# Hybrid diffusion trunk on one core: thirteen up blocks of each layer by seven products, their weight sums by adding transfers, and modulation vectors made beside merge and output projection

## The chip, the core and the metric

The kernel runs on one core of a Trainium2 chip. The core has a matrix engine (TensorE; PE in the profile, and PEld for its loading of weights), a vector engine (VectorE; DVE), a scalar engine (ScalarE; ACT), a general engine (GpSimd; POOL) and a queue that issues transfers (SyncE; SP), all running side by side and waiting for one another by semaphores. The metric is the device time of one run in microseconds; less is better.

## The reference, cut to what matters

There are 640 tokens of 1024 channels: 128 of a context (segment 0, modulated by `c_ctx`) and 512 latent ones (segment 1, modulated by `c`). Two layers do this (cut):

```
mods = silu(cond) @ w_ada[l] + b_ada[l]              # sh1, sc1, g1, sh2, sc2, g2: 6 x 1024, per segment
hn   = rmsnorm(x, norm1_g) * (1 + sc1) + sh1
f, q, k, v, gates = split(hn @ w_in)
a_four = real(fft2(f)) @ w_fourier                   # 512 -> 1024
a_attn = subln(diff_attention(q, k, v)) @ w_attn     # 1024 -> 1024
x  = x + g1 * ((sigmoid(gates)[:D] * a_four + sigmoid(gates)[D:] * a_attn) @ w_o)
hn = rmsnorm(x, norm2_g) * (1 + sc2) + sh2
u  = dwconv3(hn @ w_up, conv_w, conv_b)              # 1024 -> 2 x 2816, then 3 taps over the tokens
x  = x + g2 * ((silu(u[gate half]) * u[value half]) @ w_down)
```

All of it is float32.

## The kernel before, in words

**Layout and precision.** Channels lie on the 128 partitions and tokens on the free axis: a tile of x is 128 channels x 640 tokens, and there are eight. All large products go over float32 values that are split into a high part and a low part: `split` writes a tile's high part on ACT and its low part on DVE. One k step of an output tile is then three products for each half of the tokens (320 columns): high by high, high by low, low by high. One such product is a line `MATMUL ... 128x320` in the profile.

**Weights.** All weights of both layers are one stream of blocks in the order in which they are used (`make_plan`): `wf` (Fourier projection), `wa` (attention projection), `wo` (output projection), `up` (2 x 11 in each layer: g = 0 the value half, g = 1 the gate half, j = 0 to 10, two output tiles each), `dn` (down projection). A block of 1 MB lies in one of two buffers `w_raw` and is loaded by SP (`pump_loads`) when the block two ahead of it has been split. `queue_split` cuts it into pieces of 512 columns: ACT casts the high part into one of eight buffers `w_h`, DVE subtracts it into `w_l`. The pieces are emitted one at a time between the products (`tick`), no more than eight ahead.

**Blocks by seven products.** An ordinary up block makes two output tiles over two halves of the tokens in 2 x 2 x 8 x 3 = 96 products. Seen as a 2 x 2 matrix of quarters (`r11`, `r12`, `r21`, `r22`: output tile by half of k) it can be done in seven products of quarters instead of eight: 7 x 4 x 3 = 84. `seven` does this, with sums of `hn` tiles that are made once in a layer (`sums`) and with sums of weight quarters that `queue_split` makes for each block: `s3` = r11 + r21, r21 += r22, `s2` = r21 + r11, and later s2 += r12: four additions of DVE. Then DVE and ACT combine the seven results (`r0`, `r1`). `seven(l, g, j)` tells which blocks go this way: before, in layer 1, those of g = 0 with j of 3 and up. A layer that has such blocks is `fast`: its convolution goes over all 640 tokens in two taps, with the edge at token 128 mended by ACT.

**Down rounds.** When some up blocks are done, the finished tiles of the hidden layer are multiplied with their part of w_down (`FF_ROUNDS`: from which tile, and how many; `FF_AFTER`: behind which j). Layer 0 has three rounds (8, 6 and 8 tiles), layer 1 four (4, 6, 6 and 6). The last round of a layer is skewed with the norm of the next.

**Modulation vectors.** w_ada comes in blocks of eight k steps. `ada_open(upto, rate)` allows blocks up to a number and sets how many steps are done at each `tick`; `ada_load` has SP load 256 KB into a ring of four tiles; a step (`ada_step`) is two `SCALAR_TENSOR_TENSOR` operations of DVE, 128 x 512, `acc += w * c`, one for each segment. After each pair of blocks TensorE sums over partitions (`ada_rows`) and transposes (`ada_columns`). `ada_until` does at once what is left. The numbers `ADA_UPTO` say for each layer up to which block this goes beside the gate projection, and up to which beside the up projection.

**The norm between output projection and up projection.** `w_o` and `up_first` overlap: the second half of the tokens' output projection runs while the first half's norm is made, and the first up block is done on the first half while the second half's norm is made. For each half: sums of squares on ACT and DVE, their sum on TensorE, `ms` on DVE, `rs` = ms ** -0.5 on POOL (L597), rows of it on TensorE, then for each of the eight tiles a multiplication, on POOL the modulation (L632), and the split.

**What sets the order.** The Python code gives the order in the main. A scheduler of the tile framework then orders the instructions of each engine, and puts in the waits for tiles; buffers named `slot` come from a pool of 61.

Of the kernel before, what the change touches and what calls it, by code (L numbers as in the profile page):

```python
# [34 lines left out]
ADA_UPTO = ((6, 14), (20, 20))  # L35
ADA_RATE = (.85, .25)
FF_ROUNDS = (((0, 8), (8, 6), (14, 8)), ((0, 4), (4, 6), (10, 6), (16, 6)))
FF_AFTER = ((4, 7, 10), (2, 5, 8, 10))


def seven(l, g, j):

    return l == 1 and g == 0 and j >= 3
# [37 lines left out]
def make_plan():  # L81
# [16 lines left out]
    for l in range(DEPTH):  # L98
        kq(l, 0)
        v(l, 0)  # L100
        for h in range(8):
            if h < 7:
                kq(l, h + 1)
                if h < 6 and h % 2 == 0:
                    v(l, h // 2 + 1)
            else:
                for i in range(2):
                    w(("f", l, i), "w_in", l, 0, 8, [(256 * i, 256)])
        for i in range(4):
            for g in range(2):  # L110
                w(("g", l, g, i), "w_in", l, 0, 8, [(3584 + 1024 * g + 256 * i, 256)])
        for i in range(2):
            w(("wf", l, i), "w_fourier", l, 0, 4, [(512 * i, 512)])
        for i in range(4):
            w(("wa", l, i), "w_attn", l, 0, 8, [(256 * i, 256)])
        for i in range(4):
            w(("wo", l, i), "w_o", l, 0, 8, [(256 * i, 256)])

        def up(j):
            for g in range(2):  # L120
                add(("up", l, g, j), "s" if seven(l, g, j) else "w", "w_up", l, 0, 8, [(DFF * g + 256 * j, 256)])

        def down(r):
            m0, n = FF_ROUNDS[l][r]
            for i in range(4):
                w(("dn", l, r, i), "w_down", l, 128 * m0, n, [(256 * i, 256)])

        for j in range(11):
            up(j)
            if j in FF_AFTER[l]:  # L130
                down(FF_AFTER[l].index(j))
# [67 lines left out]
class Kern:  # L199
# [123 lines left out]
    def pump_loads(self, upto=None):  # L323
        while self.loaded < (upto or self.n) and (self.loaded < 2 or self.done[self.loaded - 2]):
            i = self.loaded
            n = self.plan[i][2][0] * self.plan[i][2][1]
            src = self.I["w_stream"][self.woff[i]:self.woff[i + 1]].rearrange("(p n) -> p n", n=n)
            self.nc.sync.dma_start(out=self.raw[i % 2][:, 0:n], in_=src)
            self.loaded += 1

# [8 lines left out]
    def queue_split(self, j):  # L339
# [19 lines left out]
        if self.plan[i][3] == "s":  # L359
            r11, r12, r21, r22 = (raw[:, 512 * q:512 * q + 512] for q in range(4))  # L360
            s3, s2 = (t[:, 0:512] for t in self.st)

            def plus(out, a, b, g):
                self.split_q.append((g, lambda: nc.vector.tensor_add(out=out, in0=a, in1=b)))

            part(g0, r11)
            plus(s3, r11, r21, g0 + 1)
            plus(r21, r21, r22, g0 + 1)
            plus(s2, r21, r11, g0 + 1)
            part(g0 + 1, s2)  # L370
            part(g0 + 2, s3)
            plus(s2, s2, r12, g0 + 3)
# [751 lines left out]
    def up(self, l, j, hn):  # L1124
        yv = {}
        for g in range(2):
            W = self.begin("up", l, g, j)
            if g and j in FF_AFTER[l] and self.fast:
                self.bg.extend(self.split_early(l, FF_AFTER[l].index(j)))
# [85 lines left out]
    def ff_split(self, l, r):  # L1215

        m0, n = FF_ROUNDS[l][r]
# [5 lines left out]
    def split_early(self, l, r):  # L1223

        m0, n = FF_ROUNDS[l][r]
# [14 lines left out]
    def down_last(self, l, after_a):  # L1240
        r = len(FF_ROUNDS[l]) - 1
# [231 lines left out]
    def layer(self, l, hn, hooks_b):  # L1473
# [74 lines left out]
        self.ada_open(ADA_UPTO[l][0], ADA_RATE[0])  # L1548
# [22 lines left out]
        self.finish_a(l, 1)  # L1571
        Z = self.merge(l)
# [3 lines left out]
        self.ada_open(ADA_UPTO[l][1], ADA_RATE[1])  # L1576
        self.ff = [None] * NFF
        if self.fast:
            self.st = [self.alloc(), self.alloc()]
# [3 lines left out]
        for j in range(1, 11):  # L1583
# [4 lines left out]
            if j in FF_AFTER[l][:-1]:  # L1588
                self.ada_until(8)
                self.down(l, FF_AFTER[l].index(j))  # L1590
        for pr in hn2:
            self.give(*pr)
        if self.fast:
            self.give(*self.st)
            for pr in self.t13 + self.t24:
                self.give(*pr)
        if l + 1 < DEPTH:
            self.ada_until(ADA_UPTO[l][1])
# [53 lines left out]
```

## Time and profile before

| | |
|---|---|
| median of 3 runs | 2190.96 us (2189.55 to 2192.48) |
| profiled execution: its own time | 2191.04 us |
| its span, first to last instruction | 2189.3 us |
| mean granted clock of TensorE | 0.994 of full speed |
| TensorE busy | 2139.6 us, 98% of the span |
| DVE busy | 1439.9 us, 66% |
| ACT busy | 988.2 us, 45% |
| POOL busy | 236.0 us, 11%, 348 instructions |
| HBM read | 194.64 MB |

The time is that of the whole run; the span leaves out the little that lies around the instructions. Busy shares are averages over stages with different limits. Stages are found in the trace by the weight blocks: each product names its weight buffer, so the first product of a block is known from the order of the plan.

### The profile page before, as it was taken

To read this page: it belongs to the slowest core of one execution; us is meant where nothing else is said; L and a number is where in the kernel's file an instruction comes from. 1 tells how busy PE (TensorE), PEld (TensorE's weight loads), DVE (VectorE), ACT (ScalarE), POOL (GpSimd) and SP (SyncE) were. 2 spreads that over 40 slices of the span, in tenths; PEclk is the share of its full clock that TensorE was granted. 3 is DMA by queue.
4 is the path that set the end of the run, shared out by engine and by line. 5 is a ranking of instruction groups with operands and counts; after the bars stand their busy time and mean duration, and the time that the engine had idled before them with its cause. 6 is when DMAs were issued, how large, how long until landed. Compare 5 with 4: busy or idle time off the path is not lost.

```text
span 2189.3 us, 36833 instructions
## 1 busy us (share of the span) xinstructions
PE 2139.6 (98%) x14766; PEld 2077.3 (95%) x14766; DVE 1439.9 (66%) x2562; ACT 988.2 (45%) x2015; POOL 236.0 (11%) x348
## 2 busy tenths in 40 slices
PE   8999999999999999999999999999999999999997
PEld 5999989999999999999999999899999999999997
DVE  5776678744479856655466776695544776857574
ACT  4665654342245423323356666543422563525352
POOL 2122222000030000000041222120000300000001
PEclk9999999999999999999999999999999999999998
DMA  8211114522234423232211111154222122222221
GB/s 319 71 51 59 48 41 153 171 82 77 91 117 140 136 97 120 93 106 92 78 68 66 45 48 56 60 159 158 78 78 77 54 84 76 78 78 82 73 78 49
DMA packets 59787, 201.74 MB, mean 92 GB/s; under 512 B 6624, under 2 KB 14176, under 8 KB 44768
## 3 DMA queue, kind: packets, MB, share of 16 engines
q1 hardware_dynamic: 59616, 199.39, 27.2%
q8 instruction: 116, 1.90, 0.4%
q14 instruction: 55, 0.45, 0.1%
HBM read 194.64 MB, written 4.72 MB: 91 GB/s over the span
## 4 chain that ended last, share of the span: by engine, by line
PE 78%; DVE 7%; ACT 6%; POOL 5%; issue 4%; DMA 1%; SPq 0%; ACTq 0%; DVEq 0%; POOLq 0%
PE ps_d L296 43%; PE ps_s L296 17%; PE ps_t L296 17%; ACT slot L188 4%; DVE slot L188 3%; POOL ors L858 2%; PE ps_t L300 2%; POOL slot L632 2%; DVE nm L188 1%; DVE on L188 1%; ACT junk L188 1%; POOL oms L857 1%; DVE w_l L188 1%; ACT w_h L188 0%; POOL slot L890 0%
## 5 line engine op out<-in xcount | busy, mean ns | idle before, releaser
L296 PE MATMUL ps_d<-slot,w_h 128*128 128x320 f32 x4984 | 983.1, 311 | 4.3 <-DVE slot L188 4.2
L296 PEld LDWEIGHTS ps_d<-slot,w_h 128*128 128x128 f32 x4984 | 787.5, 188 | 15.5 <-DVE slot L188 7.2
L296 PE MATMUL ps_d<-slot,w_l 128*128 128x320 f32 x2492 | 596.3, 309 | 1.7 <-DVE w_l L188 1.6
L188 ACT CAST w_h<-w_raw 128x512 fp32r<-128x512 f32 x520 | 318.8, 621 | 461.4 <-PE ps_d L296 240.2
L188 DVE TENSOR_TENSOR w_l<-w_raw,w_h 128x512 fp32r<-128x512 f32 x520 | 354.6, 690 | 153.4 <-ACT w_h L188 150.4
L296 PEld LDWEIGHTS ps_d<-slot,w_l 128*128 128x128 f32 x2492 | 423.2, 188 | 2.3 <-DVE w_l L188 2.3
L188 DVE TENSOR_TENSOR slot<-slot,slot 128x640 f32<-128x640 f32 (+5 forms) x339 | 240.1, 715 | 100.2 <-ACT slot L188 70.2
L296 PE MATMUL ps_t<-slot,w_h 128*128 128x320 f32 x1384 | 277.5, 309 | 0.6 <-DVE slot L188 0.3
L296 PE MATMUL ps_s<-slot,w_h 128*128 128x320 f32 x1376 | 264.9, 309 | 0.0
L296 PEld LDWEIGHTS ps_t<-slot,w_h 128*128 128x128 f32 x1384 | 221.1, 187 | 7.0 <-issue 2.5
L296 PEld LDWEIGHTS ps_s<-slot,w_h 128*128 128x128 f32 x1376 | 218.8, 188 | 0.8 <-issue 0.8
L188 DVE SCALAR_TENSOR_TENSOR slot<-slot,c_cond,slot 128x512 f32<-128x512 f32 x280 | 199.0, 746 | 29.5 <-DMA slot<-in_w_ada 20.2
L188 ACT ACTIVATE slot<-ps_s,nm 128x640 f32<-128x640 f32 (+1 forms) x160 | 113.6, 710 | 161.2 <-DVE nm L188 160.1
L296 PE MATMUL ps_t<-slot,w_l 128*128 128x320 f32 x692 | 175.4, 308 | 0.0
L296 PE MATMUL ps_s<-slot,w_l 128*128 128x320 f32 x688 | 164.2, 308 | 0.0
L188 ACT ACTIVATE slot<-slot 128x640 f32<-128x640 f32 (+2 forms) x132 | 85.1, 647 | 144.2 <-DVE slot L188 141.9
L188 DVE TENSOR_REDUCE nm<-ps_s 128x1 f32<-128x640 f32 (+1 forms) x160 | 113.8, 711 | 50.3 <-PE ps_s L296 43.8
L188 ACT CAST slot<-slot 128x640 fp32r<-128x640 f32 (+1 forms) x156 | 112.4, 726 | 49.5 <-DVE slot L188 47.4
L296 PE MATMUL ps_s<-slot,slot 128*128 128x320 f32 (+2 forms) x592 | 114.7, 318 | 5.5 <-ACT slot L188 4.7
L296 PEld LDWEIGHTS ps_t<-slot,w_l 128*128 128x128 f32 x692 | 120.1, 187 | 0.0
L296 PEld LDWEIGHTS ps_s<-slot,w_l 128*128 128x128 f32 x688 | 117.3, 188 | 0.0
L597 POOL TENSOR_TENSOR rs<-ms,c_mh 128x3 f32<-128x3 f32 (+1 forms) x9 | 8.6, 955 | 951.8 <-DVE ms L188 951.8
(142 smaller groups left out, 2199.1 us busy)
## 6 DMA issues: line engine op xcount, KB each, us to landing
w_raw<-in_w_stream SPq DMA_DIRECT2D x116, 1024.0 KB, 4.9
slot<-in_w_ada SPq DMA_DIRECT2D x160, 256.0 KB, 2.9
w_raw<-in_w_stream SPq DMA_DIRECT2D x16, 768.0 KB, 4.3
slot<-in_w_first SPq DMA_DIRECT2D x32, 256.0 KB, 6.3
slot<-in_x_t SPq DMA_DIRECT2D x8, 320.0 KB, 5.6
slot<-in_t_big SPq DMA_DIRECT2D x10, 256.0 KB, 4.1
out_y_t<-slot SPq DMA_DIRECT2D x8, 320.0 KB, 2.2
w_raw<-in_w_stream SPq DMA_DIRECT2D x4, 512.0 KB, 3.7
```

The source lines that it names most:

```text
L188: return f(*a, **kw)
L296: return self.nc.tensor.matmul(**a)
L300: return self.nc.tensor.transpose(*a)
L597: nc.gpsimd.tensor_tensor(out=rs[:, 0:n], in0=ms[:, 0:n], in1=self.mh[:, 0:n], op=ALU.pow)
L632: (eng or nc.gpsimd).tensor_scalar(out=tmp[:, a:b], in0=tmp[:, a:b], scalar1=A, scalar2=B, op0=ALU.mult, op1=ALU.add)
L857: nc.gpsimd.tensor_scalar(out=ms, in0=ss, scalar1=1.0 / 128, scalar2=EPS, op0=ALU.mult, op1=ALU.add)
L858: nc.gpsimd.tensor_tensor(out=rs, in0=ms, in1=self.mh[:, 0:1], op=ALU.pow)
```

## The change

It has four parts. In each layer 13 blocks go by seven products: those of g = 0 with j of 3 and up, and those of g = 1 with j of 3, 4, 6, 7 and 9. Their weight sums are no longer made by DVE from the loaded block: `sum_weights`, called where the block's load is issued, has SP load r11 once more into s2 and s3, and has POOL issue four transfers that add as they arrive (`accum_op`): r22 to the loaded r21, r21 to s3, r21 to s2, r22 to s2. The two sum tiles are doubled, as the weight buffers are. One addition (s2 += r12) stays on DVE. Layer 0 is now `fast` also, and takes layer 1's four down rounds. The second part of the modulation blocks is opened ahead of `merge`, at .85 steps a tick in layer 0 and .3 in layer 1, and is done by the end of `w_o`; nothing of it stands beside the up blocks any more.

```
-ADA_UPTO = ((6, 14), (20, 20))
-ADA_RATE = (.85, .25)
-FF_ROUNDS = (((0, 8), (8, 6), (14, 8)), ((0, 4), (4, 6), (10, 6), (16, 6)))
-FF_AFTER = ((4, 7, 10), (2, 5, 8, 10))
+ADA_UPTO = ((6, 12), (18, 20))
+ADA_RATE = ((.85, .85), (.85, .3))
+FF_ROUNDS = ((0, 4), (4, 6), (10, 6), (16, 6))
+FF_AFTER = (2, 5, 8, 10)
 def seven(l, g, j):
-    return l == 1 and g == 0 and j >= 3
+    return g == 0 and j >= 3 or j in (3, 4, 6, 7, 9)
...
-            self.nc.sync.dma_start(out=self.raw[i % 2][:, 0:n], in_=src)
+            raw = self.raw[i % 2]
+            self.nc.sync.dma_start(out=raw[:, 0:n], in_=src)
+            if self.plan[i][3] == "s":
+                self.sum_weights(i, raw, src)
             self.loaded += 1
+
+    def sum_weights(self, i, raw, src):
+
+        nc = self.nc
+        r11, r12, r21, r22 = (slice(512 * q, 512 * q + 512) for q in range(4))
+        s3, s2 = (t[:, 0:512] for t in self.st[i % 2])
+        for t, q in ((s2, r11), (s3, r11)):
+            nc.sync.dma_start(out=t, in_=src[:, q])
+        for t, q in ((raw[:, r21], r22), (s3, r21), (s2, r21), (s2, r22)):
+            nc.gpsimd.dma_start(out=t, in_=src[:, q], accum_op=ALU.add)
...
-            s3, s2 = (t[:, 0:512] for t in self.st)
-
-            def plus(out, a, b, g):
-                self.split_q.append((g, lambda: nc.vector.tensor_add(out=out, in0=a, in1=b)))
...
+            s3, s2 = (t[:, 0:512] for t in self.st[i % 2])
...
             part(g0, r11)
-            plus(s3, r11, r21, g0 + 1)
-            plus(r21, r21, r22, g0 + 1)
-            plus(s2, r21, r11, g0 + 1)
             part(g0 + 1, s2)
             part(g0 + 2, s3)
-            plus(s2, s2, r12, g0 + 3)
+            self.split_q.append((g0 + 3, lambda: nc.vector.tensor_add(out=s2, in0=s2, in1=r12)))
             part(g0 + 3, r21)
...
-        self.ada_open(ADA_UPTO[l][0], ADA_RATE[0])
+        self.ada_open(ADA_UPTO[l][0], ADA_RATE[l][0])
...
         self.finish_a(l, 1)
+        self.ada_open(ADA_UPTO[l][1], ADA_RATE[l][1])
         Z = self.merge(l)
...
         hooks = self.w_o(l, Z, hn2)
-        self.ada_open(ADA_UPTO[l][1], ADA_RATE[1])
+        self.ada_until(ADA_UPTO[l][1])
...
         if self.fast:
-            self.st = [self.alloc(), self.alloc()]
+            self.st = [[self.alloc(), self.alloc()] for _ in range(2)]
...
-                self.ada_until(8)
```

TensorE's list has 13,947 instructions after and 14,163 before. What the change does to the order of instructions is shown at three places.

The first is POOL's list between the two halves of layer 0's second norm: the modulation of the first half (`slot` tiles, 128 x 128 and 128 x 192), then `rs` of the second half, then its modulation (128 x 320). Before:

```order
L632 TENSOR_SCALAR slot26_6577<-slot26_6577,c_a01_81,c_mods0_78 128x128 [waits PE_49,Activation_49]
L632 TENSOR_SCALAR slot26_6577<-slot26_6577,c_a01_81,c_mods0_78 128x192 [waits Activation_49]
L632 TENSOR_SCALAR slot27_6584<-slot27_6584,c_a01_81,c_mods0_78 128x128 [waits Activation_49]
L632 TENSOR_SCALAR slot27_6584<-slot27_6584,c_a01_81,c_mods0_78 128x192 [waits Activation_49]
L597 TENSOR_TENSOR rs_6747<-ms_6746,c_mh_75 128x3 [waits DVE_49]
L632 TENSOR_SCALAR slot18_6770<-slot18_6770,c_a01_81,c_mods0_78 128x320 [waits Activation_49]
```

Of the same place after, where `slot50` and `slot40` are the two s2 tiles and `slot31` and `slot34` the two s3 tiles (lines L342, L604 and L639 are the adding transfer, `rs` and the modulation):

```order
L639 TENSOR_SCALAR slot32_6758<-slot32_6758,c_a01_81,c_mods0_78 128x128 [waits PE_49,Activation_49]
L639 TENSOR_SCALAR slot32_6758<-slot32_6758,c_a01_81,c_mods0_78 128x192 [waits Activation_49]
L342 DMA slot50_6853<-in_w_stream 128x512 [waits DMAHW7_49,PE_49]
L639 TENSOR_SCALAR slot36_6765<-slot36_6765,c_a01_81,c_mods0_78 128x128 [waits Activation_49]
L639 TENSOR_SCALAR slot36_6765<-slot36_6765,c_a01_81,c_mods0_78 128x192 [waits Activation_49]
L342 DMA slot50_6853<-in_w_stream 128x512 [waits DMASW0_49]
L342 DMA slot40_6851<-in_w_stream 128x512 [waits DMAHW1_49,DVE_49]
L342 DMA slot31_6850<-in_w_stream 128x512 [waits DMAHW2_49]
L342 DMA slot34_6852<-in_w_stream 128x512 [waits DMAHW3_49,DVE_49]
L342 DMA slot40_6851<-in_w_stream 128x512 [waits DMASW2_49]
L604 TENSOR_TENSOR rs_6934<-ms_6933,c_mh_75 128x3 [waits DVE_49]
L639 TENSOR_SCALAR slot12_6713<-slot12_6713,c_a01_81,c_mods0_78 128x320 [waits Activation_49]
```

Six transfers of two blocks' sums have moved in between, and the second addition into a tile waits there for the landing of the first (`DMASW`).

The second place is DVE's list in the attention projection of layer 0: `slot45` and `slot47` are attention gates that are multiplied with a projected tile `ps_d`, `slot28` and `slot48` the sums Z, `w_l3` a weight split. Before:

```order
L188 TENSOR_TENSOR slot45_4452<-slot45_4452,ps_d_5675 128x640 [waits PE_49]
L188 TENSOR_TENSOR w_l3_103<-w_raw0_90,w_h3_95 128x512 [waits Activation_49]
L188 TENSOR_TENSOR slot28_4276<-slot28_4276,slot45_4452 128x640 [waits DVE_49]
L188 TENSOR_TENSOR slot31_5748<-slot28_4276,slot23_5747 128x640 [waits Activation_49]
L188 TENSOR_TENSOR slot47_4727<-slot47_4727,ps_d_5730 128x640 [waits PE_49]
```

And after, where the rows with `c_cond` are modulation steps:

```order
L188 TENSOR_TENSOR slot45_4452<-slot45_4452,ps_d_5715 128x640 [waits PE_49]
L188 TENSOR_TENSOR w_l3_103<-w_raw0_90,w_h3_95 128x512 [waits Activation_49]
L188 TENSOR_TENSOR slot28_4276<-slot28_4276,slot45_4452 128x640 [waits DVE_49]
L188 SCALAR_TENSOR_TENSOR slot17_5952<-slot29_5346,c_cond_77,slot17_5952 128x512
L188 SCALAR_TENSOR_TENSOR slot57_5951<-slot39_5343,c_cond_77,slot57_5951 128x512 [waits DMAHW5_49]
L188 TENSOR_TENSOR slot16_5796<-slot28_4276,slot38_5795 128x640 [waits Activation_49]
L188 SCALAR_TENSOR_TENSOR slot17_5952<-slot39_5343,c_cond_77,slot17_5952 128x512 [waits DVE_49]
L188 SCALAR_TENSOR_TENSOR slot57_5951<-slot13_5344,c_cond_77,slot57_5951 128x512 [waits DMAHW6_49,DVE_49]
L188 SCALAR_TENSOR_TENSOR slot17_5952<-slot13_5344,c_cond_77,slot17_5952 128x512 [waits DVE_49]
L188 SCALAR_TENSOR_TENSOR slot57_5951<-slot33_5345,c_cond_77,slot57_5951 128x512 [waits DMAHW7_49,DVE_49]
L188 TENSOR_TENSOR slot47_4727<-slot47_4727,ps_d_5778 128x640 [waits PE_49]
```

Between two tiles of the projection DVE now has six such steps.

The third place is DVE's list where a seven block's weights are split. Before (layer 1; `slot37` is s2, `slot14` and `slot59` are tiles of the convolution, `slot4` and `slot5` of x):

```order
L188 TENSOR_TENSOR w_l4_104<-w_raw0_90,w_h4_96 128x512 [waits PE_49,Activation_49]
L188 TENSOR_TENSOR w_raw0_90<-w_raw0_90 128x512
L188 SCALAR_TENSOR_TENSOR slot5_127<-ps_d_18222,c_mods1_79,slot5_127 128x128 [waits PE_49]
L188 SCALAR_TENSOR_TENSOR slot5_127<-ps_d_18222,c_mods1_79,slot5_127 128x512
L188 TENSOR_TENSOR slot37_17330<-w_raw0_90 128x512 [waits DVE_49]
L188 TENSOR_TENSOR w_l5_105<-slot37_17330,w_h5_97 128x512 [waits Activation_49]
L188 TENSOR_TENSOR slot37_17330<-slot37_17330,w_raw0_90 128x512 [waits DVE_49]
```

And after (layer 0; `slot50` is s2, `slot34` s3, `slot36` and `slot58` take the combined products):

```order
L188 TENSOR_TENSOR w_l7_107<-w_raw1_91,w_h7_99 128x512 [waits DMAHW4_49,Activation_49]
L188 TENSOR_TENSOR w_l0_100<-slot50_6853,w_h0_92 128x512 [waits DMASW1_49,PE_49,Activation_49]
L188 TENSOR_TENSOR slot50_6853<-slot50_6853,w_raw1_91 128x512 [waits DVE_49]
L188 TENSOR_TENSOR slot36_7968<-slot36_7968,ps_s_7966 128x320 [waits PE_49,Activation_49]
L188 TENSOR_TENSOR w_l1_101<-slot34_6852,w_h1_93 128x512 [waits DMASW4_49,Activation_49]
L188 TENSOR_TENSOR slot58_7969<-ps_t_7967,slot36_7968 128x320 [waits DVE_49,PE_49]
L188 TENSOR_TENSOR w_l2_102<-w_raw1_91,w_h2_94 128x512 [waits DMASW7_49,Activation_49]
```

The additions ahead of the split of s2 are gone, and the splits of s2, s3 and r21 wait for a POOL transfer's landing instead.

## Rows read from the trace of the kernel before

**Rows 1.** The page: TensorE's busy time, and the last chain's shares by engine.

```profile
PE 2139.6 (98%) x14766; PEld 2077.3 (95%) x14766; DVE 1439.9 (66%) x2562; ACT 988.2 (45%) x2015; POOL 236.0 (11%) x348
...
PE 78%; DVE 7%; ACT 6%; POOL 5%; issue 4%; DMA 1%; SPq 0%; ACTq 0%; DVEq 0%; POOLq 0%
```

**Rows 2.** Stretches, layer 0: length, busy by engine, clock, DMA share, GB/s.

```profile
726.68:742.40 15.72, 15.72 (x110) 14.68 (x110) 14.55 (x26) 7.33 (x12) 0.00 (x0) 1.00 0.48 139
756.46:784.62 28.16, 28.16 (x195) 28.16 (x193) 23.54 (x41) 11.39 (x18) 0.00 (x0) 1.00 0.44 150
```

**Rows 3.** Stretches: layer 1's eight seven blocks (PE, PEld, DVE, ACT, POOL).

```profile
1858.82:1871.34 12.52, 12.52 (x86) 12.33 (x85) 10.48 (x18) 6.37 (x13) 0.00 (x0) 1.00 0.41 151
...
2007.88:2020.65 12.77, 12.77 (x86) 12.34 (x85) 9.53 (x16) 6.49 (x13) 0.00 (x0) 1.00 0.17 63
...
sum 101.46, PE 101.46 PEld 98.67 DVE 81.20 ACT 48.70 POOL 0.00; mean PE 12.68 PEld 12.33 DVE 10.15 ACT 6.09 POOL 0.00
```

**Rows 4.** Stretches: output projection to second up pair; layer 0's first up block.

```profile
604.10:684.40 80.30, 76.66 (x506) 75.91 (x505) 66.81 (x127) 40.15 (x72) 21.55 (x26) 0.96 0.37 119
633.60:656.30 22.70, 19.06 (x111) 18.31 (x110) 16.25 (x32) 8.96 (x17) 11.15 (x15) 0.85 0.41 139
1686.30:1761.60 75.30, 74.57 (x506) 73.09 (x505) 54.82 (x104) 41.55 (x84) 21.85 (x26) 1.00 0.21 71
```

**Rows 5.** TensorE's waits, 633 to 660: total us, times, longest.

```profile
PE ps_s L296 <- POOL rs L597: 2.8, 1, 2.8
```

**Rows 6.** POOL's timeline at the second norms of both layers (start, duration).

```profile
623.03 1.29 POOL L597 TENSOR_TENSOR rs<-ms,c_mh 128x3 f32<-128x3 f32 x1 [243.17 <-DVE ms L188]
...
1710.00 11.26 POOL L632 TENSOR_SCALAR slot<-slot,c_a,c_mods 128x128 f32<-128x128 f32 x16 [4.23 <-ACT slot L188]
1725.75 0.86 POOL L597 TENSOR_TENSOR rs<-ms,c_mh 128x3 f32<-128x3 f32 x1 [4.49 <-DVE ms L188]
```

**Rows 7.** Timeline, 1105 to 1128: one issue of SP.

```profile
1111.26 0.33 SPq L665 DMA_DIRECT2D slot<-in_k_t  x1
```

**Rows 8.** The page: transfers, KB each, median us from issue to landing.

```profile
w_raw<-in_w_stream SPq DMA_DIRECT2D x116, 1024.0 KB, 4.9
slot<-in_w_ada SPq DMA_DIRECT2D x160, 256.0 KB, 2.9
...
slot<-in_w_first SPq DMA_DIRECT2D x32, 256.0 KB, 6.3
```

**Rows 9.** Stretch: merge and first half of layer 0's output projection.

```profile
491.00:604.10 113.10, 113.10 (x775) 113.09 (x773) 54.83 (x79) 28.62 (x46) 0.00 (x0) 1.00 0.24 82
```

**Rows 10.** DVE by shape, 491 to 633.6: busy us, mean ns, idle before.

```profile
L188 DVE TENSOR_TENSOR w_l<-w_raw,w_h 128x512 fp32r<-128x512 f32 x36 | 24.7, 690 | 14.0 <-ACT w_h L188 14.0
L188 DVE TENSOR_TENSOR slot<-slot,slot 128x640 fp32r<-128x640 f32 x12 | 9.8, 823 | 3.2 <-ACT slot L188 3.2
L188 DVE SCALAR_TENSOR_TENSOR slot<-slot,c_cond,slot 128x512 f32<-128x512 f32 x13 | 9.3, 742 | 1.6 <-ACT slot L188 1.6
```

**Rows 11.** Stretch of layer 1's first up blocks, where DVE is fullest.

```profile
1738.70:1763.70 25.00, 24.79 (x168) 24.29 (x167) 24.95 (x41) 21.11 (x43) 0.02 (x1) 1.00 0.27 88
```

**Rows 12.** DVE by shape, 352.5 to 491: modulation steps beside the gates.

```profile
L188 DVE SCALAR_TENSOR_TENSOR slot<-slot,c_cond,slot 128x512 f32<-128x512 f32 x79 | 55.7, 745 | 11.7 <-DMA slot<-in_w_ada 8.6 <-ACT slot L188 3.0
```

**Rows 13.** DVE by shape, 1832 to 2130, layer 1's up stage.

```profile
L188 DVE TENSOR_TENSOR w_l<-w_raw,w_h 128x512 fp32r<-128x512 f32 x91 | 62.5, 687 | 20.9 <-ACT w_h L188 20.1
L188 DVE SCALAR_TENSOR_TENSOR slot<-slot,c_vecs,slot 128x639 f32<-128x639 f32 x32 | 27.5, 881 | 0.5
...
L188 DVE TENSOR_TENSOR slot<-slot,ps_t 128x320 f32<-128x320 f32 x24 | 11.6, 485 | 7.5 <-PE ps_t L296 7.5
```

**Rows 14.** TensorE's waits, 1056 to 1150, layer 0's last down round.

```profile
PE ps_d L296 <- DVE slot L188: 1.8, 4, 0.7
```

**Rows 15.** DVE by shape, 1106 to 1126, the norm of layer 1.

```profile
L188 DVE TENSOR_TENSOR slot<-slot,slot 128x320 fp32r<-128x320 f32 x8 | 4.5, 568 | 3.1 <-POOL slot L632 3.1
...
L188 DVE TENSOR_TENSOR slot<-slot,slot 128x320 f32<-128x320 f32 x3 | 1.5, 488 | 0.1
```

More of the change, by code (lines that the diff above doesn't have):

```diff
@@ L123, in down @@
         def down(r):
-            m0, n = FF_ROUNDS[l][r]
+            m0, n = FF_ROUNDS[r]
             for i in range(4):
@@ L129, in make_plan @@
             up(j)
-            if j in FF_AFTER[l]:
-                down(FF_AFTER[l].index(j))
+            if j in FF_AFTER:
+                down(FF_AFTER.index(j))
     return plan
@@ L1127, in up @@
             W = self.begin("up", l, g, j)
-            if g and j in FF_AFTER[l] and self.fast:
-                self.bg.extend(self.split_early(l, FF_AFTER[l].index(j)))
+            if g and j in FF_AFTER and self.fast:
+                self.bg.extend(self.split_early(l, FF_AFTER.index(j)))
             if seven(l, g, j):
@@ L1215, in ff_split @@
     def ff_split(self, l, r):
-        m0, n = FF_ROUNDS[l][r]
+        m0, n = FF_ROUNDS[r]
         self.flush()
@@ L1223, in split_early @@
     def split_early(self, l, r):
-        m0, n = FF_ROUNDS[l][r]
+        m0, n = FF_ROUNDS[r]
         return [lambda m=m: self.ff.__setitem__(m, self.split(self.ff[m])) for m in range(m0, m0 + min(n, 4))]
@@ L1240, in down_last @@
     def down_last(self, l, after_a):
-        r = len(FF_ROUNDS[l]) - 1
+        r = len(FF_ROUNDS) - 1
         X, n = self.ff_split(l, r)
@@ L1587, in layer @@
             self.up(l, j, hn2)
-            if j in FF_AFTER[l][:-1]:
-                self.ada_until(8)
-                self.down(l, FF_AFTER[l].index(j))
+            if j in FF_AFTER[:-1]:
+                self.down(l, FF_AFTER.index(j))
         for pr in hn2:
@@ L1593, in layer @@
         if self.fast:
-            self.give(*self.st)
+            self.give(*self.st[0], *self.st[1])
             for pr in self.t13 + self.t24:
@@ L1597, in layer @@
         if l + 1 < DEPTH:
-            self.ada_until(ADA_UPTO[l][1])
             self.tables()
```

## The prediction

> **What bounds the kernel now.** I read the page first: TensorE is busy for 98% of the span and 78% of the last chain is its matmuls [rows 1]. So time goes away only where matmuls go away or where TensorE waits; another engine matters where it comes near 100% of a stretch. Next I cut the span at the first product of each weight block, and asked the table of stretches. Two ordinary up blocks, (0,0,4) and (0,1,4), take 28.16 us without a wait [rows 2]: 192 products of 320 columns, 146.7 ns each, 14.08 us a block. A block by seven products has 84 of them, 12.32 us by that price; the eight of layer 1 take 12.52 to 12.77, mean 12.68 [rows 3]. So a seven block saves 1.40, not 1.76: 0.36 goes in small waits between its products.
>
> **Part 1, the products.** Before, 8 blocks go by seven; after, 13 in each layer, 18 more. They remove 18 x 12 = 216 products: 216 x 0.1467 = **-31.7 us**. The small waits come with them: 18 x 0.36 = **+6.5**. Both are read off existing blocks, so the pair has a narrow bound: -31.7 if the moved sums remove the waits, -22 if they grow by half.
>
> **Part 2, the modulation work leaves the first up blocks of layer 0.** From the second half of the output projection to the second up pair, layer 0 takes 80.3 us and layer 1 75.3, with the same 506 products [rows 4]. The difference is 5.0: TensorE waits 2.8 us for POOL's `rs` [rows 5], because DVE does modulation steps beside the norm, and in the first up block behind that wait the granted clock has a mean of 0.85 [rows 4], so part of the work runs at the 1.2 GHz level. Afterwards the steps are done before the norm: **-5.0**.
>
> But the first weight sums come to stand there. POOL's list has six accumulating transfers ahead of the second `rs`, where before there are none. In layer 1 POOL works 11.26 us on the first half, then is idle 4.49 until the `rs` input is there [rows 6]. In that gap must fit six issues and two landings (the second add into the same tile waits for the first). No row shows such a transfer. Below: an issue as short as SP's, 0.33 [rows 7], a landing of 2.9 as 256 KB of `in_w_ada` [rows 8]; two POOL operations (1.4) cover the first landing and two issues (0.7) the second: 6 x 0.33 + 1.5 + 2.2 = 5.7, so `rs` is 1.2 late. Above: an issue as long as the longest `rs`, 1.29 [rows 6], a landing of 6.3 as `in_w_first` [rows 8]: 6 x 1.29 + 4.9 + 3.7 = 16.3, 11.8 late. I take issues of 0.86, as POOL's `rs` in layer 1 [rows 6], with landings of 2.9, since the queue is quiet there: 5.2 + 1.5 + 1.2 = 7.9, 3.4 late. A 2.8 us wait at this place cost 5.0 with the clock, so 3.4 costs **+6.1** (2 to 15). Behind `rs` queue the eight POOL operations of the second half, and behind these the up products.
>
> **Part 3, the modulation work in merge and output projection.** Layer 0 now makes six blocks of it there: 84 DVE steps of 0.742 us [rows 10], 62.3 us. DVE is busy for 54.8 of that 113.1 us stretch now [rows 9]. By the order after, DVE has, from the first Fourier tile's product to the update of x[0], 63 steps, 24 `w_l` (0.690) and 37 operations on 640 columns (0.823) [rows 10]: 46.7 + 16.6 + 30.5 = 93.8 us. TensorE has seven Fourier tiles of 3.52, eight attention tiles of 7.04 and one output tile of 7.04, 88.0, and some 1.6 of modulation sums, by which block (0,0,3) is longer than 14.08 now, 15.72 [rows 2]: 89.6 us. DVE ends about 4 us behind. The last Z half comes out there: after the last tile DVE has six operations, 4.7 us, to do before the eighth k step at 6.2, so it can be 1.5 late for nothing. I take **+4** (0 to 11: nothing, since with DVE busy for 24.95 of 25 us TensorE lost 0.21 [rows 11]; 11 if its 63 steps also wait for their loads as they do beside the gates, 8.6 us in 79 steps [rows 12], 6.9 more).
> Layer 1 has two blocks there, 28 steps, 20.8 us, hidden: 54.8 + 20.8 is below 113. The sums on TensorE are the same ten pairs as before, elsewhere: 0.
>
> **Part 4, weight sums by transfer.** Of four DVE additions of 0.69 in a seven block one stays. DVE is not the bound there (81.2 of 101.5 us [rows 3]), so nothing is gained by itself; it makes room for the second seven block of a j. From the second product of block (0,0,3) to the update of x[0] behind j = 5 the order gives DVE 38 `w_l` (0.687), 35 operations on 320 columns (0.485), 24 taps (0.881) [rows 13], 12 operations on 640 columns (0.823) and 3 sums (0.690) [rows 10]: 76.2 us. TensorE has five seven blocks of 12.32, one ordinary of 14.08 and a down tile of 5.28, less the two products (3.52) before the start: 77.4. DVE is at 98%. There are four such stretches and two shorter ones. At 99.8% it went nearly without loss [rows 11], so I take **+2** in all (0 to 12).
> The sums must be in time, for DVE now waits for a transfer before it splits s2 and s3, and behind that wait stand the other splits, the combining of products and the taps, for all of which TensorE waits in turn. The load of a block is issued when the block two ahead is split; its s2 is wanted by DVE about one block and two products later, 12.3 + 3.5 = 15.8 us. The chain is the 1 MB load and two adds into s2: 4.9 + 2 x 2.9 = 10.7 [rows 8], up to 4.9 + 2 x 6.3 + 2 x 1.29 = 20.1. Lateness up to the 7 us after which a PSUM half is written again costs TensorE nothing. So it is hidden at both bounds, and costs only beyond (below).
>
> **Part 5, layer 0 has a fourth, shorter down round.** It ends with 18 products a half tile instead of 24. The norm of layer 1 has 4 x 6 x 0.1467 = 3.5 us less cover, and POOL needs 11.26 for its sixteen operations [rows 6], 1.4 for a k step where TensorE needs 0.88. TensorE already waits a little there, 1.8 us [rows 14]: **+1.7** (0 to 3.5). The two-tap convolutions of layer 0 and its token sums are those that layer 1 does now, beside a DVE at 99.8% [rows 11]: 0.
>
> **Sum**, against the profiled execution's own 2191.04 (span 2189.3 and 1.7 around it; the median of the runs is 2190.96, the same): -31.7 + 6.5 - 5.0 + 6.1 + 4 + 2 + 1.7 = -16.4, **2174.6 us**.
>
> **A rule that speaks against it.** DVE's subtraction on 320 columns takes 488 ns in rows that stand apart from POOL's work and 568 in those that wait for it [rows 15], 16% more. The Trainium skill (GPSIMD Engine Reference, 1. Specifications) says that GpSimd's SBUF interfaces are shared with VectorE and that this contends with DVE instructions that have two SBUF inputs. The row agrees with it for POOL's arithmetic; no row shows it for POOL issuing transfers.
>
> **Rivals.**
> - *All hidden.* `rs` is in time and merge absorbs its 4 us, as DVE at 99.8% did [rows 11], and the runs too: -31.7 + 6.5 - 5.0 + 1.7 = -28.5, 2162.5. Against it: six issues in a 4.49 us gap.
> - *POOL slows DVE.* If issuing does to DVE what POOL's arithmetic does [rows 15], twenty issues of 1.29 in a stretch of 98% add 16% of 26 us, 4.1, so DVE is 3 over TensorE in each of four: 12 more, 2187.
> - *`rs` at its late bound*: 9 more, 2184.
> - *DVE at 98 to 104% turns saved products into waits* by its idle before ACT's casts (20.1 us over layer 1's up stage [rows 13]): 16 more, 2190, no change.
> - *The adding transfers are slow; this ends slower.* Two blocks may take 24.6 us; chain plus 8 us of splitting must stay below, so a chain over 16.6 makes each of some 1.5 further pairs in a run later, less the 7 free. With a chain of 28 us (an add of 11 us, four times the landing of a plain load): 1.5 x 11.4 - 7 = 10 a run, four runs, 40: 2214. It decides from a chain of 24 us on.
>
> **How the numbers follow.** Forecast, with its own range 2167 to 2181: 0.45. All hidden: 0.15. Late `rs`: 0.10. POOL slows DVE: 0.10. No gain: 0.08. Slow adds: 0.12. A difference under 0.2% (4.4 us) can't be told from none: faster 0.80, same 0.08, slower 0.12. The range 2161 to 2190 leaves out the slow adds and the fastest part of the hidden case.
>
> **What would show it.** 13 blocks in each layer of 12.5 to 13 us; a wait of TensorE for POOL's `rs` of about 3.4 us in layer 0 with a fallen clock behind it, and none in layer 1; 2 to 6 us of waits near the first output projection tiles; POOL's transfers landing within 3 to 6 us. Wrong, if DVE or ACT wait for an s2 tile by more than 7 us, or if seven blocks grow beyond 13.5.

## The result and the profile after

The change makes the kernel slower: 2206.24 us (median of 4 runs, 2204.06 to 2209.04) against 2190.52 (4 runs), a ratio of 1.007 with a 95% interval of 1.0058 to 1.0082. The forecast was 2174.6, the range ended at 2190.

The page of the changed kernel, TensorE's busy time, the last chain's shares, and the new transfers (KB each, median us from issue to landing):

```profile
PE 2125.4 (96%) x14550; PEld 2061.7 (93%) x14550; DVE 1526.2 (69%) x2688; ACT 1058.7 (48%) x2227; POOL 328.9 (15%) x452
...
PE 74%; DVE 6%; ACT 6%; issue 5%; POOL 5%; DMA 4%; SPq 0%; ACTq 0%; DVEq 0%; POOLq 0%
...
slot<-in_w_stream POOLq DMA_DIRECT2D x78, 256.0 KB, 5.1
```

The 216 products are gone (TensorE has 14550 records where it had 14766 [rows 1]), yet its share fell from 98% to 96%: it waits more. DMA has 4% of the chain where it had 1%. Cutting the span at the first product of each weight block finds the waits in five blocks. The table of stretches for them, layer 0's first up block and then (0,0,4), (0,0,7), (1,0,4), (1,0,7) (length, busy of PE, PEld, DVE, ACT, POOL, granted clock, DMA share, GB/s):

```profile
639.80:670.10 30.30, 21.67 (x117) 21.14 (x114) 11.86 (x26) 6.87 (x13) 14.70 (x19) 0.77 0.61 148
793.80:815.10 21.30, 14.49 (x86) 14.23 (x85) 12.40 (x22) 9.80 (x20) 5.22 (x6) 0.84 0.75 149
923.00:943.80 20.80, 15.28 (x86) 15.02 (x86) 12.45 (x21) 9.79 (x20) 3.73 (x5) 0.84 0.73 150
1868.50:1889.30 20.80, 15.30 (x86) 15.04 (x86) 12.46 (x21) 9.79 (x20) 5.24 (x6) 0.84 0.71 151
1996.00:2016.30 20.30, 14.63 (x86) 14.38 (x85) 12.34 (x21) 9.77 (x20) 5.24 (x6) 0.83 0.75 154
```

The first of them was 22.7 us long before [rows 4]. The other four are seven blocks and should take 12.7 [rows 3]; each loses some 8 us, of which 5.5 to 6.8 is a wait and the rest the clock behind it. For 3 us behind the first of these waits the granted clock is 0.50, the level of 1.2 GHz:

```profile
803.70:806.70 3.00, 2.95 (x11) 2.95 (x12) 1.87 (x4) 1.90 (x4) 0.00 (x0) 0.50 0.77 114
```

**Who is waited for in the seven blocks.** TensorE's waits from 793 to 816 have one row, and ACT's from 793 to 804 name the transfer behind it:

```profile
PE ps_s L296 <- ACT slot L188: 6.8, 1, 6.8
```

```profile
ACT w_h L188 <- DMA slot<-in_w_stream: 6.9, 1, 6.9
```

ACT's timeline there (start, duration, instruction, in brackets the idle time before it):

```profile
794.66 0.61 ACT L188 CAST w_h<-w_raw 128x512 fp32r<-128x512 f32 x1
795.17 0.66 ACT L188 ACTIVATE edge<-slot,slot,c_vecs 128x1 f32<-128x1 f32 x2
802.75 0.62 ACT L188 CAST w_h<-slot 128x512 fp32r<-128x512 f32 x1 [6.92 <-DMA slot<-in_w_stream]
803.28 0.42 ACT L188 COPY slot<-ps_s 128x320 f32<-128x320 f32 x1
```

This is the whole mechanism. Block (0,0,4) runs. The cast at 802.75 is that of s2 of the *next* block, (0,1,4), which TensorE would need only behind 806, when the running block ends without a wait. The copy at 803.28 takes the first of the running block's seven products out of PSUM. The second of the seven goes into the other half of the same PSUM tile `ps_s`; its first k step is done ahead of the copy, and from its second k step on TensorE's list has it wait for the copy, since that wait is on the whole tile and not on the half. So TensorE stops 2.5 us into the block, after 20 of its 84 matmuls, and goes on in `ps_s` right behind the copy:

```profile
796.49 0.45 PE L296 MATMUL ps_t<-slot,w_h 128*128 128x320 f32 x2
803.75 0.90 PE L296 MATMUL ps_s<-slot,w_h 128*128 128x320 f32 x2 [6.81 <-ACT slot L188]
```

The copy could have been made at about 796, but in ACT's list it stands behind the cast, and the cast waits for a transfer: ACT waits 6.9 us, TensorE 6.8. SP's and POOL's timelines show why that transfer is late (issue times of the same block's load and of POOL's additions; the two at 788.51 and 795.06 go into s2):

```profile
779.52 0.33 SPq L329 DMA_DIRECT2D w_raw<-in_w_stream  x1
```

```profile
787.97 0.86 POOL L342 DMA_DIRECT2D w_raw<-in_w_stream  x1 [8.92 <-DVE slot L188]
788.51 1.21 POOL L342 DMA_DIRECT2D slot<-in_w_stream  x1
795.06 1.76 POOL L342 DMA_DIRECT2D slot<-in_w_stream  x2 [5.34 <-DMA slot<-in_w_stream]
```

ACT stood at the cast from 795.83, 16.3 us behind the load's issue at 779.52; s2 landed at 802.68, and the cast at 802.75 is 23.2 us behind the issue. Of these, r11 took 6.2 us from its issue at 781.85 to landing in s2, and the two additions 6.1 and 7.6.

**Who is waited for in the first up block.** TensorE's waits from 636 to 672, and POOL's timeline between the two halves of the norm, which answers to [rows 6]:

```profile
PE ps_d L296 <- POOL rs L604: 4.6, 1, 4.6
PE ps_d L300 <- ACT slot L188: 4.1, 1, 4.1
```

```profile
642.89 1.06 POOL L342 DMA_DIRECT2D slot<-in_w_stream  x1
...
649.62 2.68 POOL L342 DMA_DIRECT2D slot<-in_w_stream  x3 [4.70 <-DMA slot<-in_w_stream]
652.59 0.86 POOL L342 DMA_DIRECT2D slot<-in_w_stream  x1 [0.29 <-issue]
660.54 0.86 POOL L342 DMA_DIRECT2D slot<-in_w_stream  x1 [7.09 <-DMA slot<-in_w_stream]
661.10 1.22 POOL L604 TENSOR_TENSOR rs<-ms,c_mh 128x3 f32<-128x3 f32 x1
```

There are two waits, one of them forecast and one not. `rs` stands behind the last addition, which waited 7.09 us for the landing of the one before it into the same tile. The other, at L300, is for the transposes of the last modulation sum: TensorE has them in its list behind the block's first six matmuls and ahead of all others, and they wait for a copy on ACT.

### The profile page after: what moved, and what is told of

It reads as the page before. It is cut to its first block, busy times and chain, and to the rows that moved or that the text cites. A ratio compares the mean times of both kernels' runs of the same rounds, so it can differ in the third digit from the quotient of the medians.

```text
span 2207.3 us, 37192 instructions
## 1 busy us (share of the span) xinstructions
PE 2125.4 (96%) x14550; PEld 2061.7 (93%) x14550; DVE 1526.2 (69%) x2688; ACT 1058.7 (48%) x2227; POOL 328.9 (15%) x452
## 4 chain that ended last, share of the span: by engine, by line
PE 74%; DVE 6%; ACT 6%; issue 5%; POOL 5%; DMA 4%; SPq 0%; ACTq 0%; DVEq 0%; POOLq 0%
PE ps_d L296 42%; PE ps_s L296 16%; PE ps_t L296 15%; ACT slot L188 4%; DMA slot<-in_w_stream 3%; DVE slot L188 3%; POOL ors L865 2%; PE ps_t L300 2%; DVE nm L188 1%; POOL slot L639 1%; DMA slot<-in_w_first 1%; DVE on L188 1%; ACT junk L188 1%; DMA w_raw<-in_w_stream 1%; POOL oms L864 1%
## 5 line engine op out<-in xcount | busy, mean ns | idle before, releaser
L296 PE MATMUL ps_d<-slot,w_h 128*128 128x320 f32 x4888 | 989.2, 313 | 20.4 <-ACT slot L188 12.4
L296 PE MATMUL ps_d<-slot,w_l 128*128 128x320 f32 x2444 | 607.5, 311 | 0.5 <-DVE w_l L188 0.5
L188 DVE TENSOR_TENSOR slot<-slot,slot 128x640 fp32r<-128x640 f32 (+5 forms) x355 | 249.8, 712 | 92.6 <-ACT slot L188 61.4
L296 PE MATMUL ps_s<-slot,w_h 128*128 128x320 f32 x1376 | 285.5, 312 | 12.3 <-ACT slot L188 12.3
L296 PE MATMUL ps_t<-slot,w_h 128*128 128x320 f32 x1336 | 271.7, 311 | 0.0
L296 PEld LDWEIGHTS ps_s<-slot,w_h 128*128 128x128 f32 x1376 | 224.4, 190 | 15.6 <-ACT slot L188 14.7
L188 DVE SCALAR_TENSOR_TENSOR slot<-slot,c_cond,slot 128x512 f32<-128x512 f32 x280 | 197.6, 744 | 23.1 <-DMA slot<-in_w_ada 15.8
L296 PE MATMUL ps_s<-slot,w_l 128*128 128x320 f32 x688 | 181.8, 310 | 0.2 <-DVE w_l L188 0.2
L342 POOL DMA_DIRECT2D slot<-in_w_stream x78 | 69.5, 917 | 482.7 <-DMA slot<-in_w_stream 281.2
L188 ACT CAST slot<-slot 128x640 fp32r<-128x640 f32 (+1 forms) x164 | 117.5, 726 | 46.7 <-DVE slot L188 43.6
L296 PEld LDWEIGHTS ps_s<-slot,w_l 128*128 128x128 f32 x688 | 122.4, 189 | 0.4 <-DVE w_l L188 0.4
```

What stands on the lines that cost most here:

```text
L188: return f(*a, **kw)
L296: return self.nc.tensor.matmul(**a)
L342: nc.gpsimd.dma_start(out=t, in_=src[:, q], accum_op=ALU.add)
```

## The experiments

**Weight sums back on DVE**, all else as changed:

```
-            if self.plan[i][3] == "s":
-                self.sum_weights(i, raw, src)
...
+            plus(s3, r11, r21, g0 + 1)
+            plus(r21, r21, r22, g0 + 1)
+            plus(s2, r21, r11, g0 + 1)
```

> The changed kernel (2206.2 us) with the weight sums back on DVE, as four additions in a block; the 13 blocks a layer, the modulation work and the rounds stay as changed. Theory A (an in-order engine stands behind a late transfer at two kinds of places: POOL ahead of `rs`, ACT at a cast of s2): both waits go, 14 us in the first up block of layer 0 and 33 us in four seven blocks, but DVE gets 3 x 0.69 us more in each of 26 blocks, 54 us, in stretches that stood at 98%: about 40 us come back as seven blocks that are longer throughout (14 to 15 us). 2199 us, 2190 to 2215. Theory B (the transfers slow DVE itself, so that it is DVE that lacks time): the seven blocks lose no more than with the transfers, below 2185 us.

Measured: 2166.76 us, ratio to before 0.9889 (0.9874 to 0.9904). The waits go as theory A has it, but nothing comes back: the 26 seven blocks take 12.49 on average. Theory B's time is the nearer, by its number, but not its reason: `w_l` takes the same in both kernels, 685 ns beside the transfers and 684 without (rows of DVE by shape of the changed kernel from 768.6 to 854, and of this one from 764 to 842):

```profile
L188 DVE TENSOR_TENSOR w_l<-w_raw,w_h 128x512 fp32r<-128x512 f32 x27 | 18.3, 685 | 1.1 <-ACT w_h L188 1.0
```

```profile
L188 DVE TENSOR_TENSOR w_l<-w_raw,w_h 128x512 fp32r<-128x512 f32 x28 | 18.9, 684 | 0.3 <-ACT w_h L188 0.3
```

Nothing came back because DVE was never full, which theory A took it to be. The stretch of five seven blocks and one ordinary one, with four additions in each seven block, has DVE busy for 71.40 of 76.50 us, and TensorE for all of it. The stretch and a row of DVE's timeline show where the count went wrong:

```profile
762.00:838.50 76.50, 76.50 (x519) 75.73 (x518) 71.40 (x119) 48.02 (x99) 0.00 (x0) 1.00 0.22 73
```

```profile
645.65 2.49 DVE L188 TENSOR_TENSOR w_l<-w_raw,w_h 128x512 fp32r<-128x512 f32 x4
```

Four `w_l` in a row take 2.49 us, 0.62 each, though the recorded mean is 0.687: the next one starts before the recorded end of the one before. A sum of means counts this overlap twice.

**Transfers behind the norm.** A one-column copy from the norm's last tile into each sum tile:

```
+            for t in self.st[0] + self.st[1]:
+                self.nc.vector.tensor_copy(out=t[:, 0:1], in_=hn2[7][0][:, 639:640].bitcast(F32))
```

> The changed kernel with four one-column copies on DVE behind the second norm into the sum tiles, so that no adding transfer can stand ahead of `rs`. Theory A: layer 0's first up block goes from 30.3 us to about the 16.0 of layer 1, nothing else moves: 2192 us (2189 to 2195). Theory B: the transfers that come later collide with the up blocks behind, and at least half comes back: 2199 us or more.

Measured: 2200.08 us, 6.2 less than the changed kernel. The first up block falls from 30.3 to 22.7, not to 16.0: the wait for `rs` goes, the 4.1 us for the transposes stay. Nothing came back in the up blocks behind: the same four seven blocks wait 6.6, 5.4, 5.1 and 5.7 us. So the time is near theory B's 2199, but its reason was not seen; theory A missed because the block has a second wait.

```profile
639.00:661.70 22.70, 18.64 (x117) 18.38 (x114) 10.91 (x23) 6.53 (x13) 7.69 (x11) 0.85 0.27 92
```

**The late cast.** The next block's s2 is not cast before the fifth product of the running block is combined; the transfers stay as late as they are:

```
+            def cast():
+                if gate and self.mark is not None:
+                    nc.vector.tensor_copy(out=h[:, 0:1], in_=self.mark[:, 0:1])
+                nc.scalar.copy(out=h, in_=src)
...
-            part(g0 + 1, s2)
+            part(g0 + 1, s2, gate=True)
...
+            if i == 5:
+                post[0]()
+                post, self.shut, self.mark = post[1:], False, r0
```

> The changed kernel with ACT's cast of the next block's s2 held back until the fifth product of the running seven block has been combined (a one-column copy on DVE makes it wait), so that ACT's copy out of PSUM stands ahead of it. The transfers are as late as before. Theory A: the four blocks of 20 to 21 us become 12.4 to 13.5, some 33 us go: 2174 us (2170 to 2182). Theory B: the wait comes back as TensorE waiting for the split of s2 at the next block, or for DVE: 2195 us or more.

Measured: 2174.31 us, 31.9 less. The stretches of the same four blocks:

```profile
793.20:805.60 12.40, 12.40 (x86) 12.31 (x85) 11.87 (x22) 9.09 (x18) 3.50 (x4) 1.00 0.85 194
912.20:924.60 12.40, 12.40 (x86) 12.31 (x85) 11.88 (x22) 9.09 (x18) 3.52 (x4) 1.00 0.90 201
1850.30:1862.70 12.40, 12.40 (x86) 12.31 (x85) 11.89 (x22) 9.08 (x18) 3.49 (x4) 1.00 0.84 192
1969.30:1981.70 12.40, 12.40 (x86) 12.31 (x85) 11.89 (x22) 9.09 (x18) 3.50 (x4) 1.00 0.92 203
```

All four are at 12.4 us at the full clock, with the DMA engines busier than before. So the transfers are in time for the products; they were late only for the place that the cast had in ACT's list.

**Both edits.**

> Both edits, transfers behind the norm and the late cast. Theory A: the two add up, 14 + 33 us under the changed kernel: 2160 us (2156 to 2168), under the kernel before by about 30. Theory B: 2185 us or more.

Measured: 2166.62 us, 39.6 less than the changed kernel, where 6.2 and 31.9 make 38.1. This is also the time of DVE sums (2166.76): without the two waits, the transfers are worth as much as the additions that they replace, nothing.

**The copy on DVE** instead of ACT:

```
-            (a, b11, [lambda: nc.scalar.copy(out=r0[:, lo], in_=a)]),
+            (a, b11, [lambda: nc.vector.tensor_copy(out=r0[:, lo], in_=a)]),
```

> The changed kernel with the copy of a seven block's first product out of PSUM made by DVE instead of ACT; in DVE's list it stands ahead of the split of the late s2. The transfers are as before. Theory A (any in-order list in which the late s2 stands ahead of what frees PSUM stops TensorE): DVE's split of s2 waits for ACT's cast and holds the combination of the second product, so TensorE waits one product (1.8 us) later in each of the four blocks and the waits shrink from 5.5 to 6.8 us to about 4 to 5: 2199 us (2193 to 2204). Rival (only ACT's copy matters): the four waits go, 2174 us.

Measured: 2211.91 us (1.0098, 1.0081 to 1.0116), 5.7 more than the changed kernel. The rival falls, and so does theory A's time: the four waits are 5.2, 7.8, 4.5 and 5.7 us, 23.2 in sum where the changed kernel has 23.5, so they stay, now behind DVE. The 5.7 us more are hardly clear of noise: the intervals of the two kernels' ratios touch. In three of the four blocks DVE makes the copy in time (in (0,0,4) at 796.71), and TensorE stops some 3 us later, because DVE's combination of the second product stands behind the split of the late s2. That is theory A's mechanism. In (0,0,7) the copy itself is late: DVE stands for 8.1 us at a weight split that waits for ACT's cast, and ACT for 8.6 at the transfer. The waits of that block that matter, the longest of the four, from 936 to 960:

```profile
ACT w_h L188 <- DMA slot<-in_w_stream: 8.6, 1, 8.6
DVE w_l L188 <- ACT w_h L188: 8.1, 1, 8.1
...
PE ps_d L296 <- DVE slot L188: 7.8, 1, 7.8
```

**s2 on DVE**, r21 and s3 by transfer:

```
-        for t, q in ((s2, r11), (s3, r11)):
-            nc.sync.dma_start(out=t, in_=src[:, q])
-        for t, q in ((raw[:, r21], r22), (s3, r21), (s2, r21), (s2, r22)):
+        nc.sync.dma_start(out=s3, in_=src[:, r11])
+        for t, q in ((raw[:, r21], r22), (s3, r21)):
...
             part(g0, r11)
+            self.split_q.append((g0 + 1, lambda: nc.vector.tensor_add(out=s2, in0=r21, in1=r11)))
             part(g0 + 1, s2)
```

> The changed kernel with s2 made by DVE (r21 + r11, then + r12, two additions), and only r21 and s3 by adding transfers: two a block instead of four, none of which waits for another one's landing. ACT's cast of s2 stands ahead of its copy as in the changed kernel. Theory A (the late thing is the chain of load and two adding transfers, one after the other): the four waits go, and ahead of `rs` stand two transfers that wait for no landing, so the first up block is at 22 to 23: 2167 us (2164 to 2171). Rival (it is the traffic and the landings of any adding transfer that are late): at least half of the four waits stays, 2185 us or more.

Measured: 2178.72 us (0.9953, 0.9936 to 0.9969). The four waits go and the first up block takes 22.7 us, as theory A has it. But 12 us are missing. Some 7 of them are new waits of 1.6 to 1.9 us at blocks (0,0,6), (0,0,9), (1,0,6) and (1,0,9), the same kind of thing on DVE; the rest was not followed. Its addition s2 = r21 + r11 waits for the addition to r21 and stands ahead of a combination. The waits of DVE and of TensorE from 880 to 897:

```profile
DVE slot L188 <- DMA w_raw<-in_w_stream: 1.9, 1, 1.9
```

```profile
PE ps_t L296 <- DVE slot L188: 1.9, 1, 1.9
```

**The modulation work alone**, in the kernel before: the edits to `ADA_UPTO`, `ADA_RATE`, `ada_open` and `ada_until`, without the rest.

> The kernel before with the modulation work alone moved into merge and output projection. Theory A: merge takes the steps without a loss, and in the norm of layer 0 TensorE's wait for `rs` is only replaced by a wait for the transposes of the last modulation sum, which stand ahead of the first up block's products in TensorE's list, behind a copy of ACT (4.1 us in the changed kernel and in the run with DVE sums): the first up block stays at 22 to 23 us and the time at 2190 (2187 to 2193). Theory of the prediction: that block falls to 16, merge gets 4 us longer, 2189 to 2190: the two differ in the blocks, not in the sum.

Measured: 2196.64 us (1.0031, 1.0020 to 1.0042), slower. The first up block stays at 22.9, as theory A has it, with the clock at 0.85 as before [rows 4]; TensorE's only wait there is that of the transposes:

```profile
PE ps_d L300 <- ACT slot L188: 4.1, 1, 4.1
```

Neither theory foresaw the loss, 6.7 us against the kernel before in the same round (2189.92). 5.6 of it are in the last down tile of layer 0 and the first block of layer 1 (1.4 and 4.2), where TensorE waits 5.3 us for DVE from 1110 to 1150 instead of 1.8 [rows 14]. Why DVE is later there was not followed. The changed kernel has the same kind of wait at this place, 4.4 us (below).

**The modulation work finished early**, on the kernel with DVE sums:

```
                 self.later(epi)
+            self.ada_until(ADA_UPTO[l][1])
```

> DVE sums (as in the run with DVE sums, 2166.8 us), and the rest of the modulation steps, with their sums and transposes, made at once behind the first block of the output projection, so that no transposes stand beside the norm. Theory A: layer 0's first up block goes from 22.75 to about the 16.0 of layer 1: 2160 us (2158 to 2163). Rival: the wait is not that of the transposes but of the norm's own chain with DVE: 2165 to 2169, the block still over 20.

Measured: 2163.04 us, 3.7 under the kernel with DVE sums. The first up block is at 16.1 and the full clock, so the wait was that of the transposes; two sums now lengthen the first half of the output projection by 5.2 in their place:

```profile
641.20:657.30 16.10, 15.91 (x111) 15.45 (x110) 11.46 (x23) 6.72 (x14) 8.84 (x13) 1.00 0.38 131
```

**All 16 blocks by seven products, DVE sums:**

```
-    return g == 0 and j >= 3 or j in (3, 4, 6, 7, 9)
+    return j >= 3
```

> As the run with the early modulation work, and all 16 blocks of a layer from j = 3 on by seven products, with DVE sums. Each of the six further blocks saves TensorE 1.7 us and gives DVE about 7.8 us more (3 splits, 8 combinations, 4 additions, at the pitch at which they follow each other). With 13, DVE is busy for 71.4 of 76.5 us in the first run of layer 0; with 16 it would need 79 in 75. Theory A: DVE becomes the bound: 2170 us (2160 to 2180), blocks of 13 us and more. Rival (DVE has room still): 2150.

Measured: 2157.84 us (0.9852, 0.9836 to 0.9868), 5.2 under the last one and the fastest of all, ahead of both kernels. DVE has room still: the six blocks of the first run have it busy for 71.52 of 75.60 us and lose 0.42 of TensorE's time.

```profile
759.30:834.90 75.60, 75.18 (x507) 74.04 (x506) 71.52 (x123) 46.67 (x95) 0.00 (x0) 1.00 0.18 64
```

**All 16 blocks, sums by transfer**, with the three remedies (behind the norm, late cast, early modulation work):

> All 16 blocks by seven products with the sums by adding transfers, the transfers held behind the norm, the late cast and the early modulation work. Theory A: DVE, with 3 additions less in a block, needs about 68 of 75 us and isn't the bound; the transfers keep up in runs of six blocks, as in the run with both edits: 2150 us (2147 to 2156). Rival: POOL's list, which waits for one transfer's landing before the next (4 in a block, about 12 us), falls behind in a run of six, TensorE waits for s2 in the fourth to sixth block: 2160 or more.

Measured: 2165.63 us, 7.8 more than with DVE sums. The time is the rival's, the place isn't: all seven blocks are at 12.4 to 12.7, and the loss lies in the first down tile behind a run (14.4 us for 10.6 behind j = 5). There the down weights' load is late beside the transfers, and ACT waits for it (826 to 836):

```profile
ACT w_h L188 <- DMA w_raw<-in_w_stream: 3.5, 2, 2.8
```

That DVE's combinations for the down product then come late is read from the waits; no run took it apart.

## Why the prediction was wrong

**The step that failed** is in part 4: "Lateness up to the 7 us after which a PSUM half is written again costs TensorE nothing. So it is hidden at both bounds". When s2 is wanted, 15.8 us behind the load's issue, was nearly right: ACT stood at the cast after 16.3. What was wrong is the free 7 us. ACT's list, fixed before the run, has that cast in front of the copy of the running block's first product, and the running block's second product already waits for this copy, not only the one that writes the same PSUM half again. The prediction looked at DVE's list; the engine that stood was ACT. So nearly all of the lateness counts: 6.9 us of ACT's waiting became 6.8 of TensorE's. The bound of the chain, 20.1 us at most, was too low also: 23.2 were seen, with 6.2 us for r11's transfer and 6.1 and 7.6 for the two additions, where 4.9 for a load and at most 6.3 for each addition had been taken. With 7 us free even these 23.2 would have cost about nothing. The lateness, which the sum put at nothing, measured 31.9 (the late cast against the changed kernel); the "+2 (0 to 12)" of part 4 was for a full DVE, of which no run showed a loss.

The rival of slow additions named this place and nearly its price (10 us in each of four runs; 8 were measured) and ended at 2214. It asked for an addition of 11 us and got 0.12; additions of 5 to 8 were enough. Its wait is the right one, its condition the wrong one, and its chance was far too low.

**Point by point:**
- *Products, -31.7, with small waits +6.5.* The products went. Where no transfer is waited for, the 26 seven blocks lose 0.17 each instead of 0.36, 4.5 us in all, only some 1.6 more than before's eight (2.9).
- *Norm, -5.0.* Did not come. The steps that kept DVE busy left, and the transposes of the last modulation sum took their place: 22.9 us in the run of the modulation work alone, 16.1 where it is finished early. TensorE's list has these transposes behind six matmuls of the first up block and ahead of the rest; the prediction had put the sums down as "the same ten pairs as before, elsewhere: 0".
- *`rs` late, +6.1.* The place and the cause were right: 6.2 from the run behind the norm, 7.7 between the two runs with the late cast. That the number fits is in part luck. Issues took 0.86 as assumed, but landings 9.6 (median of six) instead of 2.9, and `rs` came 4.9 us behind its input, `ms`, where 3.4 were forecast; each us late then cost less than assumed, as the block had the wait for the transposes as well.

```profile
655.97 0.16 DVE L188 TENSOR_SCALAR ms<-ps_d 128x3 f32<-128x3 f32 x1 [6.38 <-PE ps_d L296]
```

- *Merge, +4.* Nothing: TensorE has no wait there. DVE is busy for 108.77 of 114.80 us.

```profile
492.80:607.60 114.80, 114.80 (x788) 113.75 (x786) 108.77 (x167) 37.96 (x62) 0.00 (x0) 1.00 0.54 174
```

- *DVE at 98%.* Wrong by the overlap shown above: 0.62 us for a step of 0.69, a tenth of every such sum. With it, an estimate makes the 93.8 us in merge some 84 and the 76.2 in a run 69. So the rival "DVE turns saved products into waits" falls.
- *POOL slows DVE.* Falls: 685 against 684 ns. What the Trainium skill (GPSIMD Engine Reference, 1. Specifications) says of the interfaces shared with VectorE stands for POOL's arithmetic [rows 15]; no run here shows it for issuing.
- *Last round, +1.7 (0 to 3.5).* The last down tile and the first block of layer 1 together are 0.6 longer than before, though the down tile has 24 products, 3.5 us, fewer: the term measured 4.1, above its bound. TensorE waits 4.4 us for DVE there instead of 1.8 [rows 14]. The run of the modulation work alone has such a wait without the shorter round, so the shorter cover need not be the reason; what makes DVE late stays open. TensorE's waits for DVE from 1110 to 1150:

```profile
PE ps_d L296 <- DVE slot L188: 4.4, 4, 3.0
```

The measured terms make -31.7 + 1.6 + 0 + 6.2 + 0 + 31.9 + 4.1 = 12.1, and the runs say 15.7. Of the 3.6 us between, 1.8 are in layer 0's norm stage without the transfers: from the third output projection block to the end of (0,1,1) the kernel with DVE sums takes 98.84 us and the kernel before 94.36, 4.5 more, of which 2.7 are two modulation sums that only moved there. About 1.9 in the profiled execution are ahead of the first product, which no part of the change touches and which isn't explained.

## What to carry to other kernels

When a result is handed from an engine to a transfer, ask not only when the consumer's consumer needs it, but where the instruction that waits for it stands in its engine's list and what is queued behind: a cast whose result was not wanted for another 12 us stopped TensorE for 7. Ask also on what a wait is: here it was on a whole PSUM tile, where the prediction had counted by halves, and that took the slack away. Sums of recorded durations overstate a busy engine; compare such a sum with the busy time of a stretch before calling the engine full. Here the cheap cure was to leave the additions where they were: DVE had the room, and with them all 16 blocks go by seven products at 2157.8 us.

## What was not expected of the hardware

An adding transfer of 256 KB takes POOL 0.86 us to issue. In the run with s2 on DVE, which has two in a block, it lands in 4.3 us (median over the run), in the changed kernel in 5.1, and in 9.6 where six of them met two loads of 1 MB and three of 256 KB. The Trainium skill (DMA: Bandwidth & Descriptors, Anatomy of one DMA — SWDGE (gpsimd) path) fits a transfer issued by GpSimd as 2.0 us plus its bytes over 436 GB/s, 2.6 us for this size as an estimate; it has no price for an adding one, and the measurement decides here. The six, from 642 to 662, and two of the run with s2 on DVE, 855 to 905 (KB each, median us to landing):

```profile
slot<-in_w_stream POOLq DMA_DIRECT2D x6, 256.0 KB, 9.6
```

```profile
slot<-in_w_stream POOLq DMA_DIRECT2D x2, 256.0 KB, 4.2
```

A wait of 5.5 to 6.8 us costs TensorE 8: in the 3 us behind each of the four the granted clock is 0.50, the level of 1.2 GHz.
